# Turning images by 180 degrees on one core: 2560 instead of 1008 columns of the second tile are turned ahead of the first tile's innermost piece

## The chip, the cores and the metric

The kernel runs on one core of a Trainium2 chip. The metric is the device time of one execution in microseconds (us). Before the change it is 122.98 us, the median of three runs that lie between 122.87 and 123.04. The profile comes from one execution that the hardware profiler recorded; times within it are counted from the start of its span.

## The reference

```python
def setup_inputs():
    batch, c, h, w = 32, 3, 256, 256
    return {"x": np.random.randn(batch, c, h, w).astype(np.float32)}

def reference(x: np.ndarray) -> np.ndarray:
    return np.rot90(x, k=2, axes=(-2, -1)).astype(np.float32)
```

Each of the 96 images of 256 x 256 float32 numbers is turned by half a turn. In an image laid out as one row of 65,536 numbers that is a reversal of the row. Nothing is computed; 25.17 MB are read and 25.17 MB written.

## The kernel before

**Tiles.** The 96 images are three groups of 32. A group fills one tile of 128 partitions by E = 16,384 columns (64 KB a partition, 8.39 MB in all): each image takes four partitions, a quarter of its row in each. The tiles are `A`, `Bt` and `Ct` for groups 0, 1 and 2; all three are in the on-chip memory at once, so no tile waits for room.

**Turning.** Reversing a row of four quarters means reversing each quarter and putting the quarters in opposite order. The order of the quarters is changed by the store, which writes them back to front (`[:, ::-1, ...]`, line 50). Each quarter is reversed in place on VectorE. `swap` (line 53) takes a piece of `w` columns from the left, and the piece of the same width that mirrors it on the right, and exchanges them reversed, with three copies: the right piece reversed into the spare tile `T`, the left piece reversed to the right, `T` to the left. `turn` (line 66) does this for a range of columns of the left half in pieces of at most J = 2,048 columns. A tile has 8,192 columns in its left half, thus four pieces of full width, and the piece next to the middle is its innermost. All copies stand at line 44 in the profile and keep the order of the program.

**Queues.** The loads (line 47) are `A` and `Ct` from SyncE's queue, called SPq in the profile and q1 in its list of DMA queues, and `Bt` from ScalarE's (ACTq, q10), which first waits for a small fill of `Bt` by VectorE (line 62). All stores (line 50) are issued from SyncE's queue, behind its loads. SyncE issues them in the order of the program and waits before each for the copies that write the columns stored.

**Order around the change**, lines 73 to 81. VectorE turns the three outer pieces of `A`. The first `LEAD` = 256 columns of `A`, final after the first of these pieces, go out in a short store of 128 KB. Then VectorE turns the first `MID` columns of `Bt`, and after that the innermost piece of `A`. Then follows the long store of `A`, columns 256 to the end, 8,064 KB; it waits for that innermost piece. VectorE goes on with the other columns of `Bt`, the store of `Bt`, the four pieces of `Ct` and the store of `Ct`.

Of the kernel before, what the change touches and what calls it, by code (L numbers as in the profile page):

```python
# [2 lines left out]

os.environ.setdefault("NEURON_RT_ULTRASERVER_MODE", "4")

# [4 lines left out]


@with_exitstack
def kernel(
    ctx: ExitStack,
    tc: tile.TileContext,
    x: bass.AP,
    out: bass.AP,
):
    nc = tc.nc  # L20
    P = 128

    B, C, H, W = x.shape
    L = H * W
    G = 32
    E = L // 4
    J = E // 8

    x4 = x.rearrange("b c h w -> (b c) (h w)").rearrange(
        "(g n) (s e) -> g (n s) e", n=G, s=4)  # L30
    o4 = out.rearrange("b c h w -> (b c) (h w)").rearrange(
        "(g n) (s e) -> g n s e", n=G, s=4)

    pool = ctx.enter_context(tc.tile_pool(name="slots", bufs=1))
    A = pool.tile([P, E], x.dtype, tag="A")
    Bt = pool.tile([P, E], x.dtype, tag="B")
    Ct = pool.tile([P, E], x.dtype, tag="C")
    T = pool.tile([P, J], x.dtype, tag="T")

    def back(t, lo, hi):  # L40
        return t[:, hi - 1:(lo - 1 if lo else None):-1]

    def copy(dst, src):
        tc.keep_in_program_order(nc.vector.tensor_copy(out=dst, in_=src))  # L44

    def load(t, g, lo, hi, queue=nc.sync):
        return queue.dma_start(out=t[:, lo:hi], in_=x4[g][:, lo:hi])

    def store(t, g, lo, hi):
        return nc.sync.dma_start(  # L50
            out=o4[g][:, ::-1, lo:hi], in_=t[:, lo:hi])

    def swap(t, lo, w):
        hi = E - lo - w
        copy(T[:, 0:w], back(t, hi, hi + w))
        copy(t[:, hi:hi + w], back(t, lo, lo + w))
        copy(t[:, lo:lo + w], T[:, 0:w])

    MID = 1008
    LEAD = 256  # L60
    load(A, 0, 0, E)
    nc.vector.memset(Bt[:, 0:256], 0.0)  # L62
    load(Bt, 1, 0, E, nc.scalar)
    load(Ct, 2, 0, E)

    def turn(t, lo, hi):
        while lo < hi:
            w = min(J, hi - lo)
            swap(t, lo, w)
            lo += w  # L70

    half = E // 2
    turn(A, 0, half - J)
    store(A, 0, 0, LEAD)
    turn(Bt, 0, MID)
    turn(A, half - J, half)
    store(A, 0, LEAD, E)
    turn(Bt, MID, half)
    store(Bt, 1, 0, E)
    turn(Ct, 0, half)  # L80
    store(Ct, 2, 0, E)


# [1 line left out]
_INS = ['x']  # L85
_OUTS = [((32, 3, 256, 256), 'float32')]


# [23 lines left out]
```

## Time and profile before

| what | value |
|---|---|
| time, median of three runs | 122.98 us |
| span of the profiled execution, first to last instruction | 121.1 us |
| time of the median outside that span | 1.88 us |
| VectorE busy | 44.9 us in 40 instructions, 37% |
| queue q1 (loads of A and Ct, all stores) | 41.94 MB, 81.3% of 16 engines' span |
| queue q10 (load of Bt) | 8.39 MB, 16.0% |
| load of A lands | 39.5 us (0.73 + 38.8) |
| store of Ct issued, lands | 85.49, 120.3 us (85.49 + 34.8) |

The profiled execution's own time is listed by its span alone. The page gives for each engine its busy time and the number of its instructions; a DMA-issuing instruction is not busy time. In the list of issues the last number is the time from an issue to the landing of the last byte, which includes the time in the queue. In the timeline each row begins with the start and the length in us. In a table of stretches each row has the stretch and its length, the busy time of the engines that compute, the granted clock, the DMA share and the GB/s; the last two count a packet whole in the stretch in which it starts, so the share can be above 1.

### The profile page before, as it was taken

The page shows a single profiled execution, that of the slowest core. Times are in us where ns is not written, and L with a number is a line of the kernel's source. Part 1 is how long each engine was busy: PE and PEld are TensorE (multiplying, and loading weights), DVE is VectorE, ACT ScalarE, POOL GpSimd, SP SyncE. Part 2 cuts the span into 40 slices and gives each one's busy share as a digit, 9 for nine tenths or more (in the row PEclk, how much of TensorE's full clock was granted, in tenths as well). Part 3 has the DMA queues.
Part 4 walks back from the last instruction along what each step waited for, and adds up shares of the span by engine and source line. Part 5 has one row for each costly group of instructions (what it writes and reads, how often), then busy time and mean ns, then how long its engine had stood idle before and what let it go on. Part 6 is the DMA issues. An engine that isn't in the chain of part 4 may idle for free.

```text
span 121.1 us, 97 instructions
## 1 busy us (share of the span) xinstructions
DVE 44.9 (37%) x40; POOL 0.2 (0%) x4
## 2 busy tenths in 40 slices
DVE  0000000000000999999999999999200000000000
POOL 0000000000000000000000000000000000000000
DMA  9777977897799789978999977987798779877980
GB/s 346 346 346 346 693 346 346 390 649 346 346 433 606 346 346 455 584 346 346 346 384 469 554 341 341 639 389 346 346 671 368 346 346 671 368 346 346 671 368 0
DMA packets 1008, 50.33 MB, mean 416 GB/s; under 512 B 112, under 2 KB 240, under 8 KB 240
## 3 DMA queue, kind: packets, MB, share of 16 engines
q1 hardware_dynamic: 864, 41.94, 81.3%
q10 hardware_dynamic: 144, 8.39, 16.0%
HBM read 25.17 MB, written 25.17 MB: 416 GB/s over the span
## 4 chain that ended last, share of the span: by engine, by line
DVE 37%; DMA 32%; issue 1%
DMA A<-in_x_dram 32%; DVE T L44 12%; DVE Bt L44 8%; DVE A L44 8%; DVE Ct L44 8%
## 5 line engine op out<-in xcount | busy, mean ns | idle before, releaser
L44 DVE COPY T<-A 128x2048 f32<-128x2048 f32 x4 | 4.9, 1227 | 38.5 <-DMA A<-in_x_dram 38.4
L44 DVE COPY T<-Bt 128x2048 f32<-128x2048 f32 (+2 forms) x5 | 5.1, 1014 | 0.2
L44 DVE COPY Bt<-T 128x2048 f32<-128x2048 f32 (+2 forms) x5 | 5.1, 1013 | 0.2
L44 DVE COPY Bt<-Bt 128x2048 f32<-128x2048 f32 (+2 forms) x5 | 5.1, 1013 | 0.2
L44 DVE COPY A<-T 128x2048 f32<-128x2048 f32 x4 | 4.9, 1227 | 0.1
L44 DVE COPY Ct<-Ct 128x2048 f32<-128x2048 f32 x4 | 4.9, 1227 | 0.1
L44 DVE COPY T<-Ct 128x2048 f32<-128x2048 f32 x4 | 4.9, 1227 | 0.1
L44 DVE COPY A<-A 128x2048 f32<-128x2048 f32 x4 | 4.9, 1227 | 0.1
L44 DVE COPY Ct<-T 128x2048 f32<-128x2048 f32 x4 | 4.9, 1226 | 0.1
L62 DVE MEMSET Bt<- 128x256 f32 x1 | 0.3, 272 | 0.8 <-PEq L96 0.8
L96 POOL MEMSET const-bfloat16-1.0<- 128x1 bf16 x1 | 0.1, 101 | 0.0
L96 POOL MEMSET const-uint8-127<- 128x1 uint8 x1 | 0.1, 101 | 0.0
L96 POOL MEMSET const-float32-0.0<- 128x1 f32 x1 | 0.1, 98 | 0.2 <-issue 0.2
L96 POOL MEMSET const-float32-1.0<- 128x1 f32 x1 | 0.1, 98 | 0.0
## 6 DMA issues: line engine op xcount, KB each, us to landing
out_dram<-A SPq DMA_DIRECT2D x1, 8064.0 KB, 24.9
out_dram<-A SPq DMA_DIRECT2D x1, 128.0 KB, 19.4
A<-in_x_dram SPq DMA_DIRECT2D x1, 38.8
Bt<-in_x_dram ACTq DMA_DIRECT2D x1, 43.1
Ct<-in_x_dram SPq DMA_DIRECT2D x1, 61.1
out_dram<-Bt SPq DMA_DIRECT2D x1, 30.7
out_dram<-Ct SPq DMA_DIRECT2D x1, 34.8
```

The source lines that it names most:

```text
L44: tc.keep_in_program_order(nc.vector.tensor_copy(out=dst, in_=src))
L62: nc.vector.memset(Bt[:, 0:256], 0.0)
L96: nc = _bacc.Bacc("TRN2", target_bir_lowering=False, num_devices=1)
```

## The change

`MID` is 2560 where it was 1008. Ahead of the innermost piece of `A`, VectorE turns 2,560 columns of `Bt` in pieces of 2,048 and 512, where it turned one piece of 1,008. Behind that piece, `Bt` has 5,632 columns left, in pieces of 2,048, 2,048 and 1,536; there were 7,184, in three pieces of 2,048 and one of 1,040. The number of copies is the same, 40 instructions on VectorE with the fill. The order of the issues on each queue is the same.

```diff
@@ -56,7 +56,7 @@
         copy(t[:, hi:hi + w], back(t, lo, lo + w))
         copy(t[:, lo:lo + w], T[:, 0:w])
 
-    MID = 1008
+    MID = 2560
     LEAD = 256
     load(A, 0, 0, E)
     nc.vector.memset(Bt[:, 0:256], 0.0)
```

## The prediction

> **What bounds the kernel now.** I read the page first: engine shares, DMA row, bytes.
>
> ```profile
> span 121.1 us, 97 instructions
> ...
> DVE 44.9 (37%) x40; POOL 0.2 (0%) x4
> ...
> DMA  9777977897799789978999977987798779877980
> ...
> HBM read 25.17 MB, written 25.17 MB: 416 GB/s over the span
> ```
>
> VectorE, the only engine that computes, is busy for 37% of the span; the 16 DMA engines are busy nearly throughout (the digits wobble because a packet is nearly as long as a slice and is counted where it starts). So the DMA engines set the end, and an edit to VectorE's order counts only if it changes what they do. The tile A arrives first and is turned first; the stores follow the loads in one queue. Next come the issues and the time from issue to landing.
>
> ```profile
> out_dram<-A SPq DMA_DIRECT2D x1, 8064.0 KB, 24.9
> out_dram<-A SPq DMA_DIRECT2D x1, 128.0 KB, 19.4
> ...
> Ct<-in_x_dram SPq DMA_DIRECT2D x1, 61.1
> out_dram<-Bt SPq DMA_DIRECT2D x1, 30.7
> ```
>
> The timeline of issues and of the copies around the edit:
>
> ```profile
> 0.73 0.39 SPq L47 DMA_DIRECT2D A<-in_x_dram  x1
> 1.18 0.42 SPq L47 DMA_DIRECT2D Ct<-in_x_dram  x1
> 43.28 0.64 SPq L50 DMA_DIRECT2D out_dram<-A  x1
> ...
> 50.86 0.69 DVE L44 COPY T<-Bt 128x1008 f32<-128x1008 f32 x1
> ...
> 53.02 1.23 DVE L44 COPY T<-A 128x2048 f32<-128x2048 f32 x1
> ...
> 56.79 0.55 SPq L50 DMA_DIRECT2D out_dram<-A  x1
> 56.80 1.23 DVE L44 COPY T<-Bt 128x2048 f32<-128x2048 f32 x1
> ...
> 60.58 1.23 DVE L44 COPY T<-Bt 128x2048 f32<-128x2048 f32 x1
> ...
> 70.35 0.54 SPq L50 DMA_DIRECT2D out_dram<-Bt  x1
> ```
>
> The load of Ct lands at 1.18 + 61.1 = 62.3. The short store of A, issued at 43.28, lands at 62.7: behind Ct's load, so the queue serves in order. The long store, issued at 56.79, thus waits some 5 us for its turn; the changed kernel uses up part of that wait. How much of it is slack needs the DMA engines packet by packet. In the stretches below the two last numbers count packets by their start: GB/s times length is the bytes that start there, and share times length is the mean duration of a packet when every one of the 16 engines starts exactly one.
>
> ```profile
> 0.70:1.70 1.00, 0.27 (x1) 0.00 (x0) 1.00 0.00 0
> 1.70:2.40 0.70, 0.00 (x0) 0.00 (x0) 1.00 4.32 1498
> ...
> 53.10:53.70 0.60, 0.60 (x1) 0.00 (x0) 1.00 4.03 1748
> ...
> 58.00:58.50 0.50, 0.47 (x2) 0.00 (x0) 1.00 6.71 2097
> 58.50:61.30 2.80, 2.73 (x3) 0.00 (x0) 1.00 0.00 0
> 61.30:62.40 1.10, 1.06 (x2) 0.00 (x0) 1.00 2.51 1058
> 64.00:64.75 0.75, 0.71 (x2) 0.00 (x0) 1.00 3.17 1376
> 80.60:81.40 0.80, 0.80 (x1) 0.00 (x0) 1.00 3.03 1311
> ```
>
> In 58.00:58.50, 0.50 x 2097 = 1,049 KB start: 16 packets of 65,536 bytes, one an engine, the last of Ct's load. Their mean is 0.50 x 6.71 = 3.36 us, where the packets of 53.10:53.70 took 0.60 x 4.03 = 2.42. So at the switch from loading to storing 0.94 us is lost on every engine. In 61.30:62.40 come 1.10 x 1058 = 1,164 KB: the 131 KB of the short store and 16 packets of 64,512 bytes, the first of the long one. The second packets of the long store start in 64.00:64.75, with 0.75 x 3.17 = 2.38 us each, so the first ones started at 61.62 to 62.37 if they took as long. From there on the stores run without a hole: Bt's first packets start in 80.60:81.40.
>
> **The change part by part.** The copies, by shape:
>
> ```profile
> L44 DVE COPY A<-T 128x2048 f32<-128x2048 f32 x4 | 4.9, 1227 | 0.1
> ...
> L44 DVE COPY T<-Bt 128x1040 f32<-128x1040 f32 x1 | 0.7, 702 | 0.0
> ...
> L44 DVE COPY T<-Bt 128x1008 f32<-128x1008 f32 x1 | 0.7, 685 | 0.0
> ```
>
> Removed ahead of A's innermost piece: three copies of 1008 columns, which with their gaps fill 50.86 to 53.02, 2.16 us. Put there: three of 2048, 60.58 - 56.80 = 3.78 us, and three of 512. No row has 512 columns; the slope of the rows is (1227 - 702) / 1008 = 0.52 ns a column, so one takes 685 - 496 x 0.52 = 427 ns, with the gap of (2.16 / 3 - 0.685) = 0.035 us 0.46, three 1.39. Sum: 3.78 + 1.39 - 2.16 = **3.01 us later**. The long store is issued at 56.79 + 3.01 = 59.80 instead of 56.79.
>
> Behind A's piece, Bt gets three of 2048, three of 2048 and three of 1536 instead of nine of 2048 and three of 1040. Bt keeps 8192 columns in five swaps, fifteen copies; durations are linear in columns, so the sum stays and Bt's store is still issued at 70.35. It is needed when the long store runs out, at 80.6: 10 us of cover, and Ct's turn and store are as before. SyncE waits 3.01 us longer for A's last copy; behind that wait on its queue stand only the stores of Bt and Ct, both waiting for later copies anyway. No load is issued there, no wait added.
>
> Now the cover of the long store. Its packets cannot reach the engines at once. For that there is one case of an issue into idle engines, the load of A: issued at 0.73, no packet before 1.70, all 16 first packets in 1.70:2.40 (0.70 x 1498 = 1,049 KB). That is 0.97 to 1.67 us after the issue began; a store's issue is itself longer, 0.55 against 0.39 us, which I add. The long store then reaches the engines at 59.80 + 0.16 + 0.97 to 1.67 = **60.93 to 61.63**. Until when have the engines other work? As it is, the long packets begin at 61.62 to 62.37, so the store would be 0.7 us early. Without the stretched last packet, Ct's load would end at 58.00 to 58.50 plus 2.42, that is 60.42 to 60.92, and the short store's 8 KB an engine (at 65,536 bytes in 2.42 us, 0.30) at 60.72 to 61.22: the long store would be 0.2 to 0.4 us late.
>
> In this trace the long store sits in the queue when the stretched packets start (56.79 + 0.16 + 0.97 to 1.67 = 57.92 to 58.62). I take it that the 0.94 us is an engine beginning to fetch the next transfers' data while its last load packet is still being written; of those, the short store's 8 KB explains 0.30 and the long store the rest. Taken away from that packet, the work must be done later: the first long packet then pays a filling of its own. That has no row for a store. The nearest is A's first load packet, 0.70 x 4.32 = 3.02 us against 2.42, so 0.60 us; the other end is 0, as between the stores of A and Bt, whose first packets take 0.80 x 3.03 = 2.42 us. Sum: the first long packet starts 61.62 - 60.93 = 0.69 (first engine) to 62.37 - 61.63 = 0.74 us earlier, and loses 0 to 0.60 again: -0.7 to -0.1. I take the middle, -0.4, because a store's data comes from the chip's own memory and not from HBM, so that I expect less than the load's 0.60, but hardly nothing. Nothing behind it waits for VectorE, so the shift goes through to the end: span 121.1 - 0.4 = 120.7. Around the span lie 122.98 - 121.1 = 1.88 us of the measured median; that gives **122.6 us**.
>
> The Trainium skill (DMA: Bandwidth & Descriptors, section Latency and other measured facts) puts the first byte of a DMA issued from this queue at about 600 ns; the rows above show 0.97 at the least, and the measurement decides. By the page the store would arrive at 60.4, in time for everything, and the fill would be all hidden. The same page (Rules for kernel authors) says to issue a DMA early and wait for it late, because its fixed cost then overlaps with other work: that speaks against this change and stands beside the second rival.
>
> **The rivals.** *The switch itself costs the 0.94 us.* Any store behind a load would do it, and the short one stays behind Ct's load. For it: the short store is there since 43.28, and the trace has just one switch, so the two stores' shares cannot be told apart. Against it: 8 KB an engine are 0.30 us of work, a third of the loss. Then the long packets still begin at 61.62 to 62.37, the store being 0.7 us early: no change, 122.98.
>
> *The late store pays twice.* The stretch of Ct's last packet stays, and the long store, no longer fetched ahead, pays a filling in its first packet. Place: the stretch from 61.6 to 64.0, where each engine's first long packet now takes 2.38 us and would take 2.7 to 3.3. Price: from 0.25 (the 0.7 us of earliness hides part of a fill of 0.94) over 0.60 (A's first packet) to 0.94 (the whole loss of the switch a second time); I take +0.6, 123.6. It decides as soon as fill and remaining stretch together exceed the 0.7 us won. For it: engines that run dry do pay, as the first packet shows, and there is only 0.2 us between the early end of the short store and the arrival. Against: the store's data needs no HBM read.
>
> *The change doesn't do what it says*: the long store would leave at its old time. The issue at 56.79 comes 0.02 us after A's last copy (55.54 + 1.23), so it does follow that copy; hardly possible, 122.98.
>
> **How the numbers follow.** Forecast 0.48, the switch 0.11, paid twice 0.40, no delay 0.01. About 0.2%, 0.25 us, is what a measurement of this kernel can tell from no change. The forecast's own range is 122.25 to 122.9; its part with a fill over 0.45 us lies within 0.2%, 0.06, and 0.42 is faster. The second rival is slower but for 0.02. So faster 0.42, same 0.06 + 0.11 + 0.01 + 0.02 = 0.20, slower 0.38. The range takes the forecast's from 122.25 and the second rival's up to 123.75, leaving out its upper end.
>
> **What would show it.** The long store's issue at 59.8 and Bt's at 70.35: the VectorE sum. Ct's last packets at 58.0 back at 2.4 to 2.7 us instead of 3.36, Ct landing near 61.3 instead of 62.3: the forecast's first half; unchanged, the first rival. The first long packets starting at 60.9 to 61.6 with 2.4 to 3.0 us: the second half. Second long packets later than 64.0 to 64.75 would show the second rival. The prediction is wrong if the long store's packets come over 1.9 us after its issue, or if Ct's last packets stay long although nothing but the short store is behind them.

## The result and the profile after

The changed kernel takes 122.01 us (median of four runs, 121.95 to 122.06) where the kernel before takes 122.98: a ratio of 0.992, 95% interval 0.9906 to 0.9934. The forecast had the sign; at 122.6 with a range from 122.25 it had less than half of the gain. The page after, engine shares and DMA totals:

```profile
span 120.3 us, 97 instructions
...
DVE 44.9 (37%) x40; POOL 0.2 (0%) x4
...
HBM read 25.17 MB, written 25.17 MB: 419 GB/s over the span
```

VectorE does the same 44.9 us of work. The span is 0.8 us shorter, the median 0.97. In all executions of the later runs, for which time and span are both on record, time less span is 1.74 to 1.84 us, 1.79 on average, in the kernel before as in the versions of it. The 1.88 us of the table put the median beside the span of one execution; in those runs a span of 121.1 us of the kernel before goes with 122.86 to 122.93 us. The issues of the same kernel, the last number the time from issue to landing:

```profile
out_dram<-A SPq DMA_DIRECT2D x1, 8064.0 KB, 21.0
out_dram<-A SPq DMA_DIRECT2D x1, 128.0 KB, 18.5
...
Ct<-in_x_dram SPq DMA_DIRECT2D x1, 60.2
out_dram<-Bt SPq DMA_DIRECT2D x1, 29.8
```

And its timeline around the edit:

```profile
54.69 0.43 DVE L44 COPY T<-Bt 128x512 f32<-128x512 f32 x1
...
58.60 1.23 DVE L44 COPY A<-T 128x2048 f32<-128x2048 f32 x1
59.85 0.54 SPq L50 DMA_DIRECT2D out_dram<-A  x1
```

The long store is issued 3.06 us later than before (59.85 against 56.79), and lands 0.85 us *earlier*: 59.85 + 21.0 = 80.85 against 56.79 + 24.9 = 81.7. The gain is already there when Ct's load lands, at 1.18 + 60.2 = 61.4 against 62.3. The stretches around the switch from loading to storing, after (columns as in the prediction):

```profile
57.85:59.20 1.35, 1.31 (x2) 0.00 (x0) 1.00 1.89 777
61.05:61.50 0.45, 0.41 (x2) 0.00 (x0) 1.00 5.57 2369
63.45:63.90 0.45, 0.41 (x2) 0.00 (x0) 1.00 5.30 2294
64.05:64.75 0.70, 0.70 (x1) 0.00 (x0) 1.00 0.00 0
```

The 16 last packets of Ct's load (1.35 x 777 = 1,049 KB) now take 1.35 x 1.89 = 2.55 us on average instead of 3.36. The first long packets start in 61.05:61.50. That stretch has 0.45 x 2369 = 1,066 KB, of which 16 long packets are 1,032; the rest, 33 KB, is packets of the short store, which weigh little in the share: at most 0.45 x 5.57 = 2.51 us is left for a first long packet, against 0.45 x 5.30 = 2.39 for a second. So no filling of 0.3 us appears. The single packets of the trace say it more closely. Ten engines have run dry; their first long packets start at 61.06 to 61.14 and take 2.42 to 2.43 us. On the other six the first long packet starts straight behind the short store and takes 2.38 us. The last of the six starts at 61.48, where the last of before started at 62.33: these 0.85 us are those of the landing. The second long packets start in 63.45:63.90 and none in 64.05:64.75, where before all did.

### The profile page after: what moved, and what is told of

It is laid out like the page before. It is cut to its first block, busy times and chain, and to the rows that moved or that the text cites. A ratio compares the mean times of both kernels' runs of the same rounds, so it can differ in the third digit from the quotient of the medians.

```text
span 120.3 us, 97 instructions
## 1 busy us (share of the span) xinstructions
DVE 44.9 (37%) x40; POOL 0.2 (0%) x4
## 2 busy tenths in 40 slices
DMA packets 1008, 50.33 MB, mean 419 GB/s; under 512 B 112, under 2 KB 240, under 8 KB 240
## 4 chain that ended last, share of the span: by engine, by line
DVE 37%; DMA 32%; issue 1%
DMA A<-in_x_dram 32%; DVE T L44 12%; DVE Bt L44 9%; DVE A L44 8%; DVE Ct L44 8%
## 6 DMA issues: line engine op xcount, KB each, us to landing
Ct<-in_x_dram SPq DMA_DIRECT2D x1, 60.2
```

## The experiments

Three theories stood at first. One: a fixed amount is lost in the last load packet when a store waits behind it. Two: every load packet that moves while the long store waits is slowed. Three: the switch costs the same whatever stands behind it. Later runs ask what it is in the waiting store that costs. In all runs but the one with MID 3072 the last load packets are read from the stretch 57.85:59.20, where the 16 of them start: mean duration = 1.35 x DMA share. Times are beside the kernel before on the same chip, 122.97 to 123.00.

### The long store earlier, and in steps later

```diff
-    MID = 1008
+    MID = 0        # mid0;   mid1536: 1536;   mid2048: 2048
```

> The long store is issued at 54.6 us and reaches the engines at about 55.8, a whole packet before the last packets of Ct's load start (58.0). Theory 1 (what is lost is a fixed amount, once, in the last load packet, whenever the long store is in the queue by then): the last load packets take 3.36 us as before, the time is that of before, 122.98 within 0.15. Theory 2 (every load packet that is on its way while the long store stands in the queue is slowed): the packets from 55.6 on are stretched as well, and the time is 0.5 to 0.9 us above before, some 123.7. Theory 3 (the switch costs the same whatever stands behind): 122.98, but then the runs with 1536 and 2048 show nothing either.

> Issue at 57.6 us, arrival at about 58.8, 0.4 to 0.8 us after the last load packets started. Theory 1: a fixed amount as long as the store arrives early enough to be fetched ahead: last load packets still 3.3 us, time 122.9 to 123.0. Theory 2: slowed only from the arrival on, two thirds of the 0.94 us: last packets 2.9 to 3.0 us, time about 122.6.

> Issue at 58.4 us, arrival at about 59.6, 1.1 to 1.6 us after the last load packets started, 0.8 to 1.3 before they could end. Theory 1: still 0.6 to 0.9 us lost, time 122.7 to 123.0. Theory 2: a third of the 0.94 us, last packets 2.7 us, time about 122.3.

Stretches with MID 0, where the one above the last load packets holds the packets before them:

```profile
55.40:56.80 1.40, 1.37 (x2) 0.00 (x0) 1.00 1.73 749
57.85:59.20 1.35, 1.32 (x2) 0.00 (x0) 1.00 2.59 777
```

The last load packets with 1536:

```profile
57.85:59.20 1.35, 1.31 (x2) 0.00 (x0) 1.00 2.40 777
```

With 2048, and the same again with the 2304 of a later run:

```profile
57.85:59.20 1.35, 1.31 (x2) 0.00 (x0) 1.00 2.01 777
```

The issue times of the table are those of the timelines.

| MID | long store issued | last load packets | time | ratio, 95% interval |
|---|---|---|---|---|
| 0 | 54.59 | 3.50 us | 122.95 | 1.0001 (0.999 to 1.0013) |
| 1008 (before) | 56.79 | 3.36 | 122.98 | |
| 1536 | 57.45 | 3.24 | 122.85 | 0.998 (0.9967 to 0.9993) |
| 2048 | 58.43 | 2.71 | 122.24 | 0.9948 (0.9932 to 0.9965) |
| 2304 | 59.37 | 2.71 | 122.08 | 0.992 (0.9904 to 0.9937) |
| 2560 (after) | 59.85 | 2.55 | 122.01 | 0.992 (0.9906 to 0.9934) |

With MID 0 the long store waits from about 55.8 on, but the load packets of 55.40:56.80 take 1.40 x 1.73 = 2.42 us, as all others; only the last ones are stretched, and the time is that of before. So theory two falls as a loss in every packet on its way. Theory three falls with the steps. Theory one holds with a correction: the loss stays within the last load packet, but there it isn't all or nothing. With 1536 a little of it is gone. With 2048 it is down to 0.29 us, which is the size that theory two gave for this run: the store, on the engines about 1.2 us after its issue, comes some 0.9 to 1.2 us before the last load packets can end. But with 2304, where it is issued 0.94 us later, the loss is still 0.29 us. So the loss falls with a later issue, yet not in proportion to it; why is open.

### The delay without the order

```diff
+    copy(T[:, 0:J], back(Bt, half - J, half))
+    copy(T[:, 0:J], back(Bt, half - J, half))
+    copy(T[:, 0:560], back(Bt, half - 560, half))
     turn(A, half - J, half)
     store(A, 0, LEAD, E)
```

> MID stays 1008; three more copies into the spare tile, whose result nobody reads, hold VectorE for 3.0 us ahead of A's innermost piece, so the long store is issued at 59.8 us as in the changed kernel, and the stores of Bt and Ct at 73.4 and 88.5 us, still before the queue asks for them (80.5 and 99.9). If the moment of the long store's issue is all that the change does: last load packets 2.5 to 2.7 us, time 122.0. If it is the order or the size of the pieces of Bt: 122.9 to 123.0.

It took 122.12 us, ratio 0.9924 (0.991 to 0.9939), as the changed kernel within the intervals. Its timeline has the issue at the place wanted:

```profile
60.06 0.55 SPq L50 DMA_DIRECT2D out_dram<-A  x1
```

and its last load packets take 1.35 x 1.88 = 2.54 us:

```profile
57.85:59.20 1.35, 1.32 (x2) 0.00 (x0) 1.00 1.88 777
```

So with 3 us of useless copies on VectorE the kernel is 0.85 us faster than before, because the long store leaves at 60.06. Ct's store, issued at 88.76 instead of 85.49, lands 30.9 us later, at 119.7: its lateness is covered. The moment of the issue is all that the change does; the pieces of Bt are only the clock.

### How much data stands behind the load

In the changed kernel the short store alone stands behind Ct's load while the last load packets move. Its size was varied with MID at 2560.

```diff
-    LEAD = 256
+    LEAD = 1024    # lead1024;   lead512: 512;   lead128: 128
```

> MID 2560 and a short store of 1024 columns instead of 256: 32 KB an engine, four times as much, stands behind the load of Ct, while the long store comes as late as in the changed kernel. If the loss at the switch is data that an engine fetches ahead, of whatever store, the last load packets are stretched as in the kernel of before (3.2 to 3.4 us) and the time goes up towards 122.9, or, if what was fetched ahead is won back at once, stays at 122.0 with stretched packets and a hole-free switch. If the loss belongs to the long store (its 64 KB rows), the last load packets stay at 2.5 to 2.7 us, and the time is 121.8 to 122.0, since the longer short store also covers the arrival of the long one.

> MID 2560 and a short store of 512 columns, 16 KB an engine. If the loss grows with the data that stands behind the load until an engine has taken some 30 KB of it (0.13 us lost at 8 KB, 1.10 at 32 KB): last load packets 2.8 to 2.95 us, time 122.1 to 122.4. If there is a step, by the size of the rows or whatever else: 2.56 us and 121.95, or 3.5 us and 122.9.

> MID 2560, short store of 128 columns, 4 KB an engine. By the line through 8, 16 and 32 KB (0.13, 0.45, 1.10 us lost: the transfer time of the data less 0.16) nothing is lost in the last load packets: 2.42 to 2.46 us. The short store then ends before the long one arrives at 61.06, and the hole takes the gain: time 121.95 to 122.15.

The last load packets with 1024 columns:

```profile
57.85:59.20 1.35, 1.32 (x2) 0.00 (x0) 1.00 2.61 777
```

and from the list of issues of the same kernel the short store and the load:

```profile
out_dram<-A SPq DMA_DIRECT2D x1, 512.0 KB, 20.4
...
Ct<-in_x_dram SPq DMA_DIRECT2D x1, 61.3
```

The last load packets with 512 columns:

```profile
57.85:59.20 1.35, 1.31 (x2) 0.00 (x0) 1.00 2.12 777
```

With 128 columns:

```profile
57.85:59.20 1.35, 1.32 (x2) 0.00 (x0) 1.00 1.81 777
```

| short store, KB an engine | transfer time (65.5 KB in 2.42 us) | last load packets | lost over 2.42 | time | ratio, 95% interval |
|---|---|---|---|---|---|
| 4 | 0.15 us | 2.44 | 0.02 | 122.18 | 0.9934 (0.9919 to 0.9948) |
| 8 (after) | 0.30 | 2.55 | 0.13 | 122.01 | 0.992 (0.9906 to 0.9934) |
| 16 | 0.60 | 2.86 | 0.44 | 122.31 | 0.9938 (0.9924 to 0.9953) |
| 32 | 1.21 | 3.52 | 1.10 | 122.86 | 0.9987 (0.9977 to 0.9997) |

On the mean of the engines the loss is the transfer time of what stands behind the load, less 0.11 to 0.17 us. The packets of the short store grow with it, from 512 bytes to 4,096, eight on each engine, so the amount and the size of a packet are not told apart. With 32 KB an engine nearly the whole gain of the change is gone although the long store comes as late as in the changed kernel. So the loss does not need the long store. (At 4 KB the loss is gone as expected, and the time, a little above its expected range, is put down to the hole; the first long packets start at 61.14 to 61.29 on engines that have all run dry.) And it is not won back: the short store of 32 KB lands at 43.40 + 20.4 = 63.8, Ct's load at 1.16 + 61.3 = 62.5; the 1.3 us between them is the full transfer time once more. With everything of A waiting, as with MID 0, the loss is 3.50 - 2.42 = 1.08, no more than with 32 KB: the loss stops growing at about that much (an estimate from these rows).

### Which memory it is read from

```diff
-    store(A, 0, 0, LEAD)
+    nc.sync.dma_start(out=o4[0][:, ::-1, 0:LEAD], in_=x4[0][:, 0:LEAD])
```

with MID 2560 and LEAD 1024. The first 1,024 columns of each quarter of group 0 thus go out unturned.

> MID 2560; in place of the short store stands a copy of the same 1024 columns (32 KB an engine) straight from the input in HBM to the output in HBM, queued right behind Ct's load; the first 1024 columns of each quarter of group 0 thus go out unturned. If the loss comes from reading the tile memory while the load still writes into it, the last load packets stay at 2.42 to 2.55 us, where a short store of 1024 columns made them 3.52. If any data fetched ahead behind the load costs its time, whatever memory it is read from, they take 3.3 to 3.6 us. The total depends on how long the copy's own packets take, which no row shows; only the last load packets decide.

The last load packets of this kernel:

```profile
57.85:59.20 1.35, 1.31 (x2) 0.00 (x0) 1.00 1.79 777
```

and from its list of issues the copy and the load:

```profile
out_dram<-in_x_dram SPq DMA_DIRECT2D x1, 512.0 KB, 61.1
...
Ct<-in_x_dram SPq DMA_DIRECT2D x1, 60.3
```

1.35 x 1.79 = 2.42 us: nothing is lost, with the same 32 KB an engine behind the load that cost 1.10 us when they were read from tile A. The copy lands at 1.62 + 61.1 = 62.7, 1.2 us after the load (1.16 + 60.3 = 61.5), so its own transfer is as long as the short store's. The time is 121.98, ratio 0.9915 (0.99 to 0.993), against 122.86. In both traces the 512 KB are 128 packets of 4,096 bytes that take 0.16 us each. What differs is the memory that they are read from, and the issue: the copy waits for no work of VectorE and is issued at 1.62 us, the short store at 43.40. The early issue was not tried apart; in both kernels the data stand in the queue for over 14 us before the last load packets start. So the loss goes with reading tile memory for a store that waits behind a load into tile memory. That an engine does both at once is the explanation that fits; the records don't show reads and writes apart.

### No short store, and too late

```diff
-    MID = 1008
+    MID = 2560     # no_lead;   no_lead_2304: 2304
...
-    store(A, 0, 0, LEAD)
...
-    store(A, 0, LEAD, E)
+    store(A, 0, 0, E)
```

> MID 2560 and no short store: A goes out in one store of all columns at 59.8 us. The engines have nothing behind Ct's load until it arrives at 61.06. Theory that the loss is data fetched ahead of a store: last load packets 2.42 us, not stretched at all, a hole of 0.2 to 0.7 us, first packets of the store at 61.06 with 2.42 us each, time 122.0 within 0.15. Rival, that an engine that ran dry pays a filling, as the first packet of A's load does (0.6 us): first packets about 3.0 us, time 122.3 to 122.7.

> MID 2304 and no short store: arrival at 60.65, between the ends of the first engine's load (60.4) and the last one's (60.9). The hole is 0.4 us smaller than with 2560 (122.44); the late engines' last packets are stretched by up to 0.2. Time 122.0 to 122.2. If an engine that runs dry lost time beyond the hole, it would stay at 122.3 or more.

Stretches with 2560 and no short store:

```profile
57.85:59.20 1.35, 1.32 (x2) 0.00 (x0) 1.00 1.79 777
59.20:61.10 1.90, 1.84 (x2) 0.00 (x0) 1.00 0.00 0
61.10:61.30 0.20, 0.19 (x1) 0.00 (x0) 1.00 12.29 5243
61.30:63.50 2.20, 2.17 (x2) 0.00 (x0) 1.00 0.00 0
63.50:63.80 0.30, 0.27 (x2) 0.00 (x0) 1.00 8.08 3495
```

And the last load packets with 2304 and no short store:

```profile
57.85:59.20 1.35, 1.31 (x2) 0.00 (x0) 1.00 1.80 777
```

With 2560 the last load packets take 2.42 us, undisturbed. All 16 engines start the store within 0.20 us (0.20 x 5243 = 1,049 KB), about 1.3 us after the issue at 59.84. The first packets take 0.20 x 12.29 = 2.46 us, the second 0.30 x 8.08 = 2.42: an engine that ran dry pays 0.04 us on a store, not the 0.6 that A's first load packet paid. The time, 122.44 us, ratio 0.9953 (0.9938 to 0.9968), is nevertheless above the 122.0 expected and lies in the range of the rival, whose packets of 3.0 us do not appear. The hole was priced too low. By the single packets of the trace an engine waits 0.6 us on average between its load and its store (loads end at 60.32 to 60.92, the store starts at 61.12 to 61.26), in the changed kernel 0.1 between the short store and the long one. These 0.5 us more, less the 0.13 that the load no longer loses, come near the 0.43 us over the changed kernel. With 2304 the time is 122.17, ratio 0.9934 (0.9919 to 0.9948), as expected; the last load packets take 1.35 x 1.80 = 2.43 us and are not stretched.

```diff
-    MID = 1008
+    MID = 3072     # mid3072;   mid2304: 2304
```

> With the short store of 256: issue at 60.6, arrival at 61.8 us, while the short store ends at 60.8 to 61.4. Last load packets 2.56 as in the changed kernel, a hole of 0.4 to 1.0 us, first long packets at 61.8 with 2.38 to 2.43 us. Past the point, lateness counts in full for the last engine: time 122.35 to 122.75. If the loss of before depends on anything else that a later issue relieves, it would be 122.0 or below.

> Issue at 59.4 us, arrival at about 60.65, where the short store of the changed kernel ends (60.8 to 61.4): no hole is left. If the last load packets are as in the changed kernel (2.56), the time is 121.85 to 121.95; if the earlier arrival already stretches them (2.6 to 2.7), it is 122.0 to 122.1.

MID 3072 takes 122.85 us, ratio 0.9988 (0.9974 to 1.0001), 0.1 above its expected range: past the point, lateness eats the gain. Its profile cannot be used to price the hole: it is of an execution of 123.29 us, and all its engines run late already in the loads. Its last load packets and, in the last row, its first long ones:

```profile
58.50:59.20 0.70, 0.70 (x1) 0.00 (x0) 1.00 3.64 1404
59.20:60.30 1.10, 1.07 (x2) 0.00 (x0) 1.00 0.17 60
...
61.90:62.80 0.90, 0.87 (x2) 0.00 (x0) 1.00 2.77 1177
```

The last load packets of the changed kernel:

```profile
57.80:58.55 0.75, 0.75 (x1) 0.00 (x0) 1.00 3.41 1398
```

With 3072, 0.70 x 1404 = 983 KB, 15 packets, start in 58.50:59.20 and one more, 1.10 x 60 = 66 KB, behind them, where in the changed kernel all 16 (0.75 x 1398 = 1,049 KB) start by 58.55. The first long packets, with a little of the short store, take 0.90 x 2.77 = 2.49 us at most: no filling here either. MID 2304 takes 122.08, ratio 0.992 (0.9904 to 0.9937): no better than 2560, since what it saves in holes it loses in last load packets of 2.71 us. No version that turns all of the images took less time than the changed kernel.

## Why the prediction was wrong, and where it was right

**VectorE's sum** held. The long store was forecast at 59.80 and came at 59.85, with all of the profile 0.05 later (the short store's issue stands at 43.33 instead of 43.28). The copy of 512 columns takes the 0.43 us worked out; Bt's store is issued at 70.40, and its 10 us of cover were never touched.

**The loss in the last load packets** was put in the right place. Its cause was taken to be an engine fetching a waiting store's data during its last load packet; the runs with other sizes fit that, and the copy from HBM shows in addition that the memory counts, but the reads themselves are not in the records. The short store's own share was taken as 0.30 and measured as 0.13.

**The step that failed** is the next one: "Taken away from that packet, the work must be done later: the first long packet then pays a filling of its own." I took 0.3 us for it, from 0 to the 0.60 of A's first load packet. The first packet of a store into dry engines pays 0.04 us, and on the six late engines of the changed kernel, which set the end, nothing. The load's row was the wrong neighbour: the end of the range that I called "0, as between the stores of A and Bt" was nearly the true one. What the load loses is not saved later, so nothing had to be paid back: with 32 KB the short store took its full time once more.

**The arrival** was mis-sized for the late engines. From A's load I let the store reach the engines over 0.70 us (60.93 to 61.63). Without a short store it reached them all in 61.10:61.30. So the last engines did not have to wait for it until 61.63; they went straight on from the short store, the last at 61.48. Together: -0.85 and nothing back, where the forecast had -0.7 + 0.3.

**The time outside the span** was 1.88 us in the sum and is 1.79 on average in the runs. Without the filling the forecast's own sum gives 122.28 us, inside its range; with the 0.85 for the 0.7 it is 122.13, and with 1.79 for 1.88 it is 122.04, where 122.01 was measured. So the filling is the largest error, and all three together put the result below the range.

**The rivals.** That the switch itself costs the 0.94 us is wrong for the store of 256 columns and would have been right for one of 1024: the amount behind the load decides. That the late store pays twice did not happen at 2560; by 3072 the lateness costs nearly all of the gain, but not by a filling; how much of it the hole is, no profile here shows.

**Issuing early.** The Trainium skill (DMA: Bandwidth & Descriptors, section Rules for kernel authors) advises to issue a DMA early. Here that holds only behind the best point: issued at 54.59 the store gives 122.95 us, at 59.85 it gives 122.01, at 60.95 again 122.85. The 600 ns to the first byte that the Trainium skill states (DMA: Bandwidth & Descriptors, section Latency and other measured facts) are about half of the 1.2 to 1.3 us measured here from the start of the store's issue to its first packets; from the end of the issue, 59.85 + 0.54, to the first long packet at 61.06 it is 0.67 us.

## What to carry to other kernels

Where loads into tile memory and stores out of it share the DMA engines, as here, a store that waits behind the last load is not free, even if it only waits: it lengthens the last load packets by nearly the transfer time of what waits, up to some 32 KB an engine, and then takes its full time all the same. Time its issue so that it arrives as the load ends, about 1.2 us ahead here, and bridge the gap with a small store, here 8 KB an engine. Look at the duration of single packets at the switch from loading to storing; the busy share of the DMA engines looks full in both cases (97% of the span in both queues together, before and after).

## What the runs showed of the hardware that was not expected

A waiting store costs the load's last packets its own transfer time less some 0.15 us (0.13 us at 8 KB an engine, 0.44 at 16, 1.10 at 32), and its packets then take their full time all the same. The same 32 KB read from HBM, by a copy issued earlier, cost nothing. Whether the engine really reads ahead, and why nothing is won back, is open: the records show packets, not reads and writes apart. An idle engine's first packet takes 0.04 us over the next ones on a store (no short store, 2.46 against 2.42), but 0.60 on the one load issued into idle engines.
